# A change at the start of a hybrid attention block: which load comes second, and when the first weight piece is split

## The chip, the cores and the metric

The kernel runs on one core of one Trainium2 chip. A core has five engines with an instruction stream each: TensorE (PE, matrix products; its weight loads are shown apart as PEld), VectorE (DVE), ScalarE (ACT), GpSimd (POOL) and SyncE (SP, which here only issues DMAs). They wait for each other by semaphores. The metric is the device time of one launch in microseconds (us), lower is better.

## The reference

One layer of an encoder trunk on 256 tokens of width 2048, in float32. What matters here is its beginning: the norm of the input and one large projection.

```python
u = _rms_norm(x, norm_mix_pre[l])
mix = hybrid_mixer(u, w_in[l], ...)        # begins with proj = u @ w_in
x = x + _rms_norm(mix, norm_mix_post[l])
hdn = jnp.square(jax.nn.relu(_rms_norm(x, norm_mlp_pre[l]) @ w_mlp_up[l]))
x = x + _rms_norm(hdn @ w_mlp_down[l], norm_mlp_post[l])
```

## The kernel before, in words

A float32 product is made of three faster ones. Each operand is split into a high part (a copy rounded to the type `fp32r`, made by ScalarE) and a low part (the operand minus its high part, made by VectorE); the products high x high, high x low and low x high are added up in PSUM. For x one tile `pk` of 128 x 512 holds both parts of 128 rows of x side by side (256 tokens each), so that one matmul of 512 columns against a weight's high part `whi` makes two of the products, and one of 256 columns against its low part `wlo` makes the third.

The weights come as a stream `wst` of pieces of 128 x 1024 numbers (512 KB). The part of the program that the change touches is the first projection, of three groups of 128 output columns (`qb[0]` to `qb[2]`). Each group needs two pieces: pieces 0, 2 and 4 hold the weights for the first 1024 rows of x, pieces 1, 3 and 5 those for the rest. x comes transposed as `xt`, 16 slices `k` of 128 rows x 256 tokens, into the tile `X0`.

- Loads. `loadx(a, b)` loads slices a to b-1 of x; `load(n, q)` loads half q (512 columns, 256 KB) of piece n. SyncE's queue takes them in the order of the code, except for `loadx(0, 2)` and `loadx(2, 4)`, which ScalarE issues. SyncE waits before an issue when the semaphore that it would use belongs to a load that has not landed.
- Splits. `xsplit(k)` makes the high part (ScalarE, L242) and the low part (VectorE, L243) of slice k. The two parts of x carry the norm's gain, and the norm's factor comes later. `wpart(n, q)` does it for half q of piece n (L331, L332).
- Products. `prods(n, ks, low)` issues the matmuls of piece n for the slices `ks`: those with `whi` (L340) or those with `wlo` (L338). TensorE's order is the order of the code, since it stands under a manual schedule.
- The first loop runs over q = 0, 1, each with four slices of x and half a piece of each of the three groups. In the loop the order is: two x splits, the split of piece 0, its products with those two slices, two more x splits, their products, then pieces 2 and 4.
- Ahead of it, TensorE makes seven products of a tile of zeros, `zt`, into a PSUM bank that nobody reads (L281). Each is two matmul instructions in the trace, and 14 stand there.

All later matmuls, some 8,300 of them, follow in an order fixed by the code and by a small planner. The buffers of `whi` and `wlo` turn in threes, so the first split of piece 1 (L331, L332) writes the buffers of piece 0, and waits for TensorE's last product with them.

Of the kernel before, what the change touches and what calls it, by code (L numbers as in the profile page):

```python
# [10 lines left out]
F32 = mybir.dt.float32  # L11
F32R = mybir.dt.float32r
AF = mybir.ActivationFunctionType
ALU = mybir.AluOpType
# [3 lines left out]
T = 256  # L18
# [32 lines left out]
def hybrid_block(ctx, tc, xt, x, gains, params, consts, lora, gup, wst, out):  # L51
    nc = tc.nc
    V, A, G, PE = nc.vector, nc.scalar, nc.gpsimd, nc.tensor
# [11 lines left out]
    def nm(s):  # L65
        uid[0] += 1
        return f"{s}_{uid[0]}"

    def gps():
        return pg.tile([128, 512], F32, tag="gps", name=nm("gps"), bufs=4)  # L70

    def mps():
        return pm.tile([128, 512], F32, tag="mps", name=nm("mps"), bufs=4)

    def pk():
        return pkpool.tile([128, 512], F32R, tag="pk", name=nm("pk"), bufs=24)
# [14 lines left out]
    def P(name, i=0, r=slice(0, 128)):  # L91
        return par[r, PC[name] + i:PC[name] + i + 1]
# [143 lines left out]
    def split(src, dst, scale=None):  # L236

        if scale is None:
            A.activation(dst[:, 0:T], src, AF.Copy)
            V.tensor_tensor(dst[:, T:], src, dst[:, 0:T].bitcast(F32), ALU.subtract)  # L240
        else:
            A.activation(dst[:, 0:T], src, AF.Copy, scale=scale)  # L242
            V.scalar_tensor_tensor(dst[:, T:], src, scale, dst[:, 0:T].bitcast(F32), ALU.mult, ALU.subtract)  # L243

    def rsqrt(y, m, t):

# [19 lines left out]
    X0 = rp.tile([128, KT, T], F32, tag="SC", name="x0", bufs=1)  # L266

    def loadx(a, b, queue=nc.sync):
        return queue.dma_start(out=X0[:, a:b, :], in_=xt[:, a:b, :])

    nc.sync.dma_start(out=par, in_=params)
    for a in (0, 2):
        first_x = loadx(a, a + 2, nc.scalar)
    with tc.issue_after(first_x.ins):
        warm = A.activation(dum, dum, AF.Tanh)
    A6 = rp.tile([128, 6, T], F32, tag="b6", name="a6", bufs=1)
    zt = rp.tile([128, T], F32, tag="tha", name="zt", bufs=1)
    V.memset(zt, 0.0)
    idle = mps()
    for i in range(7):  # L280
        PE.matmul(idle[:, 0:T], zt[:, 0:128], zt, start=True, stop=True)  # L281
    raws = {}

    def load(n, q=None):

        if n not in raws:
            raws[n] = (rp.tile([128, HALF], F32, tag="m", name=nm("raw"), bufs=4) if n % 2 else
                       wpool.tile([128, HALF], F32, tag="raw", name=nm("raw"), bufs=3))
        cs = slice(0, HALF) if q is None else slice(512 * q, 512 * q + 512)
        nc.sync.dma_start(out=raws[n][:, cs], in_=wst[n][:, cs])  # L290

    for n in (0, 2, 4):
        load(n, 0)
    loadx(4, 8)
    for n in (0, 2, 4):
# [20 lines left out]

    def xsplit(k):
        u = pk()
        split(X0[:, k, :], u, P("g1", k))
        upk.append(u)  # L320

    qb = [gps() for _ in range(3)]
    w = {}

    def wpart(n, q):
        if n not in w:
            w[n] = (wpool.tile([128, HALF], F32R, tag="whi", name=nm("whi"), bufs=3),
                    wpool.tile([128, HALF], F32R, tag="wlo", name=nm("wlo"), bufs=3))
        hi, lo = w[n]
        cs = slice(512 * q, 512 * q + 512)  # L330
        A.activation(hi[:, cs], raws[n][:, cs], AF.Copy)  # L331
        V.tensor_tensor(lo[:, cs], raws[n][:, cs], hi[:, cs].bitcast(F32), ALU.subtract)  # L332

    def prods(n, ks, low):
        for k in ks:
            i = k % 8
            if low:
                PE.matmul(qb[n // 2][:, 0:T], w[n][1][:, i * 128:i * 128 + 128], upk[k][:, 0:T], start=False, stop=k == 15)  # L338
            else:
                PE.matmul(qb[n // 2], w[n][0][:, i * 128:i * 128 + 128], upk[k], start=k == 0, stop=False)  # L340

    for q in range(2):
        ks = range(4 * q, 4 * q + 4)
        for k in ks[0:2]:
            xsplit(k)
        wpart(0, q)
        prods(0, ks[0:2], False)
        for k in ks[2:4]:
            xsplit(k)
        prods(0, ks[2:4], False)  # L350
        wpart(2, q)
        prods(2, ks, False)
        prods(0, ks, True)
        wpart(4, q)
        prods(4, ks, False)
        prods(2, ks, True)
        prods(4, ks, True)
    for k in range(8, 12):
        xsplit(k)
# [66 lines left out]
    def sb_mix():  # L426
# [66 lines left out]
        for h in range(4):  # L493
            ps = mps()
            PE.matmul(ps[:, 0:256], v[0][:, h * 128:h * 128 + 128], t[:, h, 0:256], start=True, stop=False)
            PE.matmul(ps[:, 128:256], v[1][:, h * 128:h * 128 + 128], t[:, h, 256:384], start=False, stop=True)
            y = pk()
            split(ps[:, 0:256], y)
            out.append(y)
            if h % 2:  # L500
                yield 2.5
        done["ya"] = out

    def fox_mix():
# [72 lines left out]
        for h in range(4):  # L577
            ps = mps()
            PE.matmul(ps[:, 0:256], v[0][:, h * 128:h * 128 + 128], pT[:, h, 0:256], start=True, stop=False)
            PE.matmul(ps[:, 128:256], v[1][:, h * 128:h * 128 + 128], pT[:, h, 256:384], start=False, stop=True)  # L580
            y = pk()
            split(ps[:, 0:256], y)
            out.append(y)
            if h % 2:
                yield 2.5
# [453 lines left out]
    c0 = g0 + 80  # L1039
# [216 lines left out]
    for k2 in range(0, KT, 2):  # L1256
        turned(k2, 1)
        src = [trs[k2 // 2][:, i * T:i * T + T] for i in range(2)]
# [342 lines left out]
    for g in range(4):  # L1601
# [8 lines left out]
        for tt, ps in enumerate(tok(hp, 3 if g == 3 else 1)):  # L1610
# [25 lines left out]
            with tc.issue_after(added.ins):  # L1636
                for c in (1024, 1536):
                    cs = slice(c, c + 512)
# [131 lines left out]
```

## Time and profile before

| what | us |
|---|---|
| median of 3 runs | 1495.75 |
| the runs | 1493.69, 1497.37, 1495.75 |
| profiled execution, first to last instruction (the span) | 1493.8 |
| TensorE busy in it | 1480.8 |

The page gives no time of the profiled execution beside its span; the span lies 1.95 us below the median of the runs and next to the lowest of them. Busy times are sums over the instructions of an engine; a matmul's row shows its latency, and matmuls overlap, so that the distance between starts is the better measure of what one costs. All the work that the change touches lies in the first 20 us.

### The profile page before, as it was taken

The page shows a single profiled execution, that of the slowest core. Times are in us where ns is not written, and L with a number is a line of the kernel's source. Part 1 is how long each engine was busy: PE and PEld are TensorE (multiplying, and loading weights), DVE is VectorE, ACT ScalarE, POOL GpSimd, SP SyncE. Part 2 cuts the span into 40 slices and gives each one's busy share as a digit, 9 for nine tenths or more (in the row PEclk, how much of TensorE's full clock was granted, in tenths as well). Part 3 has the DMA queues.
Part 4 walks back from the last instruction along what each step waited for, and adds up shares of the span by engine and source line. Part 5 has one row for each costly group of instructions (what it writes and reads, how often), then busy time and mean ns, then how long its engine had stood idle before and what let it go on. Part 6 is the DMA issues. An engine that isn't in the chain of part 4 may idle for free.

```text
span 1493.8 us, 22852 instructions
## 1 busy us (share of the span) xinstructions
PE 1480.8 (99%) x8427; PEld 1250.7 (84%) x8427; DVE 1213.1 (81%) x1688; ACT 933.9 (63%) x1396; POOL 91.3 (6%) x160
## 2 busy tenths in 40 slices
PE   9999999999999999999999999999999999999997
PEld 8888888888778888788888888888888888888885
DVE  7666677999679798567547788999899999999996
ACT  7465666664576554474444777776766776777663
POOL 0021000100001100000000000000000000000000
PEclk9999999999999999999999999999999999999999
DMA  7545455545544545445755868888888788889874
GB/s 282 188 148 191 163 170 180 172 162 198 171 153 161 184 169 209 144 151 194 269 196 204 275 213 249 255 257 259 242 232 264 238 262 248 260 248 283 259 250 151
DMA packets 107759, 317.70 MB, mean 213 GB/s; under 512 B 10752, under 2 KB 14976, under 8 KB 107392
## 3 DMA queue, kind: packets, MB, share of 16 engines
q1 hardware_dynamic: 94688, 284.39, 54.9%
q0 software_dynamic: 8064, 29.36, 10.5%
q10 hardware_dynamic: 4896, 2.49, 0.6%
q8 instruction: 66, 1.08, 0.3%
q14 instruction: 45, 0.37, 0.1%
HBM read 282.65 MB, written 4.19 MB: 192 GB/s over the span
## 4 chain that ended last, share of the span: by engine, by line
PE 96%; DVE 1%; ACT 1%; issue 1%; POOL 0%; POOLq 0%; DVEq 0%; ACTq 0%
PE gps L220 28%; PE gps L174 23%; PE gps L178 13%; PE gps L204 7%; PE mps L1478 3%; PE mps L1479 3%; PE mps L1480 3%; PE gps L1480 3%; PE gps L1478 2%; PE gps L1479 2%; PE gps L182 2%; PE gps L340 1%; PE mps L791 1%; PE mps L281 0%; PE gps L1237 0%
## 5 line engine op out<-in xcount | busy, mean ns | idle before, releaser
L159 DVE TENSOR_TENSOR wlo<-raw,whi 128x1024 fp32r<-128x1024 f32 x497 | 602.7, 1220 | 157.2 <-ACT whi L158 140.7
L158 ACT ACTIVATE whi<-raw 128x1024 fp32r<-128x1024 f32 x497 | 522.0, 1056 | 249.7 <-PE gps L220 101.1
L174 PE MATMUL gps<-pk,whi 128*128 128x512 f32 x1336 | 336.5, 391 | 0.4 <-ACT whi L158 0.4
L174 PEld LDWEIGHTS gps<-pk,whi 128*128 128x128 f32 x1336 | 247.3, 188 | 48.8 <-ACT whi L158 0.6
L220 PE MATMUL gps<-whi,pk 128*128 128x512 f32 x1136 | 286.0, 391 | 0.0
L220 PEld LDWEIGHTS gps<-whi,pk 128*128 128x128 f32 x1136 | 211.5, 188 | 44.0
L178 PEld LDWEIGHTS gps<-pk,wlo 128*128 128x128 f32 x1424 | 194.1, 190 | 14.1 <-DVE wlo L159 0.3
L178 PE MATMUL gps<-pk,wlo 128*128 128x256 f32 x1424 | 199.3, 282 | 0.0
L220 PE MATMUL gps<-wlo,pk 128*128 128x512 f32 x568 | 155.3, 392 | 0.0
L220 PEld LDWEIGHTS gps<-wlo,pk 128*128 128x128 f32 x568 | 105.7, 188 | 21.9
L1341 DVE TENSOR_TENSOR sp<-raw,sp 128x1024 fp32r<-128x1024 f32 x67 | 81.7, 1220 | 6.7 <-ACT sp L1340 6.5
L1340 ACT ACTIVATE sp<-raw 128x1024 fp32r<-128x1024 f32 x67 | 70.6, 1054 | 19.6 <-DMA raw<-in_wst_dram 6.3
L1369 ACT ACTIVATE sp<-gps 128x512 f32<-128x512 f32 x52 | 31.1, 598 | 72.1 <-PE gps L182 72.1
L204 PE MATMUL gps<-whi,pk 128*128 128x512 f32 x256 | 68.9, 390 | 0.0
L1478 PE MATMUL mps<-whi,fm 128*128 128x512 f32 x168 | 66.1, 394 | 0.0
L1479 PE MATMUL mps<-whi,fm 128*128 128x512 f32 x168 | 65.8, 392 | 0.0
L1480 PE MATMUL mps<-wlo,fm 128*128 128x512 f32 x168 | 65.5, 390 | 0.0
L1440 POOL DMA_DIRECT2D raw<-raw x40 | 34.9, 873 | 431.1 <-DVE raw L1437 111.7
L204 PEld LDWEIGHTS gps<-whi,pk 128*128 128x128 f32 x256 | 47.8, 188 | 9.9
L1480 PE MATMUL gps<-wlo,fm 128*128 128x512 f32 x126 | 49.4, 392 | 0.5 <-DVE wlo L159 0.4
L1478 PE MATMUL gps<-whi,fm 128*128 128x512 f32 x126 | 49.2, 391 | 0.0
L1437 DVE TENSOR_TENSOR raw<-raw,raw 128x1024 f32<-128x1024 f32 x40 | 48.8, 1220 | 0.4
(393 smaller groups left out, 2009.1 us busy)
## 6 DMA issues: line engine op xcount, KB each, us to landing
raw<-in_wst_dram SPq DMA_DIRECT2D x499, 512.0 KB, 4.4
raw<-raw POOLq DMA_DIRECT2D x40, 512.0 KB, 7.6
sp<-in_wst_dram SPq DMA_DIRECT2D x16, 512.0 KB, 5.4
raw<-sp POOLq DMA_DIRECT2D x8, 512.0 KB, 6.9
sp<-raw POOLq DMA_DIRECT2D x8, 512.0 KB, 7.0
x<-in_x_dram SPq DMA_DIRECT2D x8, 256.0 KB, 5.5
xs<-x SPq DMA_DIRECT2D x2, 1024.0 KB, 4.9
x<-xs SPq DMA_DIRECT2D x4, 512.0 KB, 6.2
```

Source lines behind the costliest of these rows:

```text
L158: A.activation(hi, raw, AF.Copy)
L159: V.tensor_tensor(lo, raw, hi.bitcast(F32), ALU.subtract)
L174: PE.matmul(ps, hi[:, i * 128:i * 128 + 128], pks[i], start=first and i == 0, stop=False)
L178: PE.matmul(ps[:, 0:T], lo[:, i * 128:i * 128 + 128], pks[i][:, 0:T], start=False, stop=False)
L204: PE.matmul(ps[tt], pks[k][:, c:c + 128], w[:, (k - k0) * 512:(k - k0) * 512 + 512], start=k == 0 and part == 0 and w is hl[0], stop=w is ...
L220: PE.matmul(ps[tt], pks[k][:, c:c + 128], w[:, (k - k0) * 512:(k - k0) * 512 + 512], start=k == 0 and part == 0 and w is hl[0], stop=False)
L1340: A.activation(hi, raw, AF.Copy)
L1341: V.tensor_tensor(lo, raw, hi.bitcast(F32), ALU.subtract)
L1437: V.tensor_tensor(x, x, z, ALU.add)
L1478: PE.matmul(Q[f], p, w, start=d == 0 and i == 0, stop=False)
L1479: PE.matmul(Q[f], pl, w, start=False, stop=False)
L1480: PE.matmul(Q[f], p, wl, start=False, stop=d == nd - 1 and i == 1)
```

## The change

Four edits. The load of slices 2 and 3 of x (`loadx(2, 4)`) moves from ScalarE's queue into SyncE's, behind the first half of piece 0. The high part of that half is made in two instructions of 256 columns instead of one of 512. Its low part is made after the low parts of slices 2 and 3 instead of before them (`tc.issue_after` sets that order). And four products of zeros stand where seven stood.

```diff
     nc.sync.dma_start(out=par, in_=params)
-    for a in (0, 2):
-        first_x = loadx(a, a + 2, nc.scalar)
+    first_x = loadx(0, 2, nc.scalar)
...
-    for i in range(7):
+    for i in range(4):
         PE.matmul(idle[:, 0:T], zt[:, 0:128], zt, start=True, stop=True)
...
-    for n in (0, 2, 4):
+    load(0, 0)
+    loadx(2, 4)
+    for n in (2, 4):
         load(n, 0)
     loadx(4, 8)
...
-    def wpart(n, q):
+    def whigh(n, c0, c1):
         if n not in w:
             w[n] = (wpool.tile([128, HALF], F32R, tag="whi", name=nm("whi"), bufs=3),
                     wpool.tile([128, HALF], F32R, tag="wlo", name=nm("wlo"), bufs=3))
+        A.activation(w[n][0][:, c0:c1], raws[n][:, c0:c1], AF.Copy)
+
+    def wlow(n, c0, c1):
         hi, lo = w[n]
-        cs = slice(512 * q, 512 * q + 512)
-        A.activation(hi[:, cs], raws[n][:, cs], AF.Copy)
-        V.tensor_tensor(lo[:, cs], raws[n][:, cs], hi[:, cs].bitcast(F32), ALU.subtract)
+        V.tensor_tensor(lo[:, c0:c1], raws[n][:, c0:c1], hi[:, c0:c1].bitcast(F32), ALU.subtract)
+
+    def wpart(n, q):
+        whigh(n, 512 * q, 512 * q + 512)
+        wlow(n, 512 * q, 512 * q + 512)
...
-        wpart(0, q)
-        prods(0, ks[0:2], False)
+        if q:
+            wpart(0, q)
+            prods(0, ks[0:2], False)
+        else:
+            for i in range(2):
+                whigh(0, 256 * i, 256 * i + 256)
+            prods(0, ks[0:2], False)
         for k in ks[2:4]:
-            xsplit(k)
+            lows = xsplit(k)
         prods(0, ks[2:4], False)
+        if q == 0:
+            with tc.issue_after(lows.ins):
+                wlow(0, 0, 512)
         wpart(2, q)
```

On SyncE, the first loads of the program before the change (`raw` are the weight pieces 0, 2 and 4, 512 columns of each; `x` of 128x1024 is slices 4 to 7):

```order
L271 DMA par<-in_params_dram 128x116
L290 DMA raw_101<-in_wst_dram 128x512
L290 DMA raw_103<-in_wst_dram 128x512
L290 DMA raw_105<-in_wst_dram 128x512
L269 DMA x_85<-in_xt_dram 128x1024
```

The same place now, where `x` of 128x512 is slices 2 and 3:

```order
L271 DMA par<-in_params_dram 128x116
L289 DMA raw_97<-in_wst_dram 128x512
L269 DMA x_85<-in_xt_dram 128x512
L289 DMA raw_100<-in_wst_dram 128x512
L289 DMA raw_102<-in_wst_dram 128x512
L269 DMA x_85<-in_xt_dram 128x1024
```

Slices 2 and 3 stand behind piece 0 and ahead of pieces 2 and 4; what follows keeps its order.

On VectorE, the low parts of x (`pk`) and of the weights (`wlo`) before, from slice 0 to piece 4:

```order
L243 SCALAR_TENSOR_TENSOR pk_132<-x_85,par,pk_132 128x256
L243 SCALAR_TENSOR_TENSOR pk_135<-x_85,par,pk_135 128x256
L332 TENSOR_TENSOR wlo_139<-raw_101,whi_138 128x512
L243 SCALAR_TENSOR_TENSOR pk_144<-x_85,par,pk_144 128x256
L243 SCALAR_TENSOR_TENSOR pk_147<-x_85,par,pk_147 128x256
L332 TENSOR_TENSOR wlo_153<-raw_103,whi_152 128x512
L332 TENSOR_TENSOR wlo_165<-raw_105,whi_164 128x512
```

And now:

```order
L243 SCALAR_TENSOR_TENSOR pk_129<-x_85,par,pk_129 128x256
L243 SCALAR_TENSOR_TENSOR pk_132<-x_85,par,pk_132 128x256
L243 SCALAR_TENSOR_TENSOR pk_141<-x_85,par,pk_141 128x256
L243 SCALAR_TENSOR_TENSOR pk_144<-x_85,par,pk_144 128x256
L335 TENSOR_TENSOR wlo_136<-raw_97,whi_135 128x512
L335 TENSOR_TENSOR wlo_151<-raw_100,whi_150 128x512
L335 TENSOR_TENSOR wlo_163<-raw_102,whi_162 128x512
```

The low part of piece 0 has moved behind those of slices 2 and 3; the same seven instructions stand there. On ScalarE one instruction of 512 columns has become two of 256 in the same place, ahead of slice 2. TensorE's products stand in the order in which they stood, behind four products of zeros instead of seven, and from there to the end every engine's order is as before.

## Rows read from the trace of the kernel before

**Rows 1.** The page: busy time of each engine, share of the span, instructions.

```profile
PE 1480.8 (99%) x8427; PEld 1250.7 (84%) x8427; DVE 1213.1 (81%) x1688; ACT 933.9 (63%) x1396; POOL 91.3 (6%) x160
```

**Rows 2.** The chain that ended last, first 20 us: start, length, what.

```profile
1.18 6.33 PE mps L281 x14
...
7.98 1.84 PE gps L340 x6
...
16.36 1.84 PE gps L340 x8
```

**Rows 3.** Timeline of TensorE's matmuls: start, length, engine, line, operation, operands, count.

```profile
1.77 1.49 PE L281 MATMUL mps<-zt 128*128 128x256 f32 x3
...
6.46 1.04 PE L281 MATMUL mps<-zt 128*128 128x256 f32 x2
...
13.84 0.64 PE L338 MATMUL gps<-pk,wlo 128*128 128x256 f32 x4
...
16.19 2.00 PE L340 MATMUL gps<-pk,whi 128*128 128x512 f32 x8
```

**Rows 4.** Timeline of TensorE's weight loads, with the idle time ahead of them.

```profile
7.98 0.19 PEld L340 LDWEIGHTS gps<-pk,whi 128*128 128x128 f32 x1 [0.44 <-DVE pk L243]
8.37 1.01 PEld L340 LDWEIGHTS gps<-pk,whi 128*128 128x128 f32 x5 [0.21 <-DVE pk L243]
```

**Rows 5.** Timeline of ScalarE, from its first issues to slice 4 of x.

```profile
0.73 0.90 ACTq L269 DMA_DIRECT2D x<-in_xt_dram  x2
...
3.65 0.91 ACT L242 ACTIVATE pk<-x,par 128x256 fp32r<-128x256 f32 x2 [0.49 <-DMA x<-in_xt_dram]
6.17 0.63 ACT L331 ACTIVATE whi<-raw 128x512 fp32r<-128x512 f32 x1 [1.61 <-DMA raw<-in_wst_dram]
...
8.73 0.91 ACT L242 ACTIVATE pk<-x,par 128x256 fp32r<-128x256 f32 x2
```

**Rows 6.** Timeline of VectorE, from slice 0 of x to slice 15.

```profile
4.19 0.89 DVE L243 SCALAR_TENSOR_TENSOR pk<-x,par,pk 128x256 fp32r<-128x256 f32 x2 [0.51 <-ACT pk L242]
6.84 0.69 DVE L332 TENSOR_TENSOR wlo<-raw,whi 128x512 fp32r<-128x512 f32 x1 [1.76 <-ACT whi L331]
7.45 0.88 DVE L243 SCALAR_TENSOR_TENSOR pk<-x,par,pk 128x256 fp32r<-128x256 f32 x2
...
12.83 1.68 DVE L243 SCALAR_TENSOR_TENSOR pk<-x,par,pk 128x256 fp32r<-128x256 f32 x4
...
15.79 1.67 DVE L243 SCALAR_TENSOR_TENSOR pk<-x,par,pk 128x256 fp32r<-128x256 f32 x4
```

**Rows 7.** DMA issues, one issue each in four narrow windows: count, size, us to landing.

```profile
x<-in_xt_dram ACTq DMA_DIRECT2D x1, 256.0 KB, 2.9
...
raw<-in_wst_dram SPq DMA_DIRECT2D x1, 256.0 KB, 5.0
...
x<-in_xt_dram ACTq DMA_DIRECT2D x1, 256.0 KB, 5.2
...
x<-in_xt_dram SPq DMA_DIRECT2D x1, 512.0 KB, 6.1
```

**Rows 8.** Timeline of SyncE's issues (each `x3` has three, 0.46 apart).

```profile
1.18 1.37 SPq L290 DMA_DIRECT2D raw<-in_wst_dram  x3
2.59 0.43 SPq L269 DMA_DIRECT2D x<-in_xt_dram  x1
```

**Rows 9.** Narrow timelines of TensorE: the product of slice 2, and two weight loads.

```profile
7.98 0.50 PE L340 MATMUL gps<-pk,whi 128*128 128x512 f32 x1
...
17.35 0.41 PEld L340 LDWEIGHTS gps<-pk,whi 128*128 128x128 f32 x2
```

**Rows 10.** VectorE's wait ahead of line 332 between 13 and 15 us: ns min/median/max, start.

```profile
L332 DVEq EVENT_SEMAPHORE  x1: 859/859/859, 13.7 to 13.7; - x1
```

**Rows 11.** Table of stretches: length, busy us of the engines, PEclk, DMA share, GB/s.

```profile
1.18:7.51 6.33, 6.33 (x15) 5.01 (x16) 1.99 (x7) 3.73 (x8) 1.53 (x6) 1.00 0.89 293
...
8.38:19.00 10.62, 10.62 (x63) 9.36 (x63) 10.55 (x22) 9.88 (x22) 0.00 (x0) 1.00 1.03 421
```

More of the change, by code (lines that the diff above doesn't have):

```diff
@@ L242, in split @@
             A.activation(dst[:, 0:T], src, AF.Copy, scale=scale)
-            V.scalar_tensor_tensor(dst[:, T:], src, scale, dst[:, 0:T].bitcast(F32), ALU.mult, ALU.subtract)
+            return V.scalar_tensor_tensor(dst[:, T:], src, scale, dst[:, 0:T].bitcast(F32), ALU.mult, ALU.subtract)
     def rsqrt(y, m, t):
@@ L318, in xsplit @@
         u = pk()
-        split(X0[:, k, :], u, P("g1", k))
+        done_low = split(X0[:, k, :], u, P("g1", k))
         upk.append(u)
+        return done_low
     qb = [gps() for _ in range(3)]
     w = {}
-    def wpart(n, q):
+    def whigh(n, c0, c1):
         if n not in w:
```

## The prediction

> **What bounds the kernel now.** First the page: TensorE is busy for 1480.8 us of a span of 1493.8 [rows 1]. Only its first microseconds and the writing of the output stand outside. Then the chain of waits over the first 20 us: it runs through TensorE alone, from the zero products at 1.18 (6.33 us) to the third real product at 7.98 and on, without leaving the engine [rows 2]. Whoever wants to move the end by work at the start must move TensorE's own queue.
>
> So I read how TensorE stands to those who feed it. Its weight loads wait twice, 0.44 us ahead of slice 2's product and 0.21 ahead of slice 3's, both for the low part of x [rows 4]. Behind 8.38 it is busy for all of the stretch to 19.00 [rows 11], and for 99% of the span [rows 1]. A shift at 8.37 therefore reaches the end, unless somebody who feeds TensorE can't follow.
>
> Two such feeders are near. ScalarE starts slice 4 at 8.73 [rows 5], which is when its load lands: issue at 2.59 plus 6.1 [rows 7, 8]. Behind that, the DMA engines are full (share 1.03, 421 GB/s [rows 11]). VectorE is busy for 10.55 us of the 10.62 from 8.38 to 19.00 [rows 11]: a second queue as tight as TensorE's.
>
> **The change, part by part.**
>
> *The load order.* Piece 0's first half lands at 1.18 + 5.0 = 6.2, and ScalarE waits 1.61 us for it [rows 5, 7, 8]. Slices 2 and 3, 256 KB too, ran beside it from ScalarE's queue, issued at about 1.2 and landed after 5.2, at 6.4 [rows 5, 7]. Now piece 0 has only slices 0 and 1 and the small parameters beside it. What lands when it goes alone no row shows. Bounds: 6.2 (nothing gained), and 4.5, which is slices 0 and 1's landing (0.73 + 2.9 = 3.6 [rows 5, 7]) plus 256 KB at the stretch's 293 GB/s, 0.9 us [rows 11]. I take 5.2, in the middle. Slices 2 and 3 have the same bytes ahead as before; I take 6.3, bounds 5.9 and 6.5.
>
> *The high part in halves.* No ACTIVATE of 128x256 without a scale is in these rows; two with one take 0.91 for a pair, 512 columns 0.63 [rows 5]. So the pair costs 0.6 to 0.9, up to 0.3 more. It begins at 5.2, and ScalarE is idle until 6.3; cost 0. If piece 0 came at 6.2 after all, these 0.3 would delay slice 2.
>
> *The low part later.* This is where the gain is. Slice 3's low part now ends at 7.45 + 0.88 = 8.33, since VectorE makes piece 0's low part first, from 6.84 [rows 6]. Afterwards slice 2's low part begins 0.54 after its high part (4.19 against 3.65 [rows 5, 6]): 6.3 + 0.02 + 0.54 = 6.86, and the pair ends 0.88 later at 7.74. That is 0.59 earlier, and slice 3's product is released at 7.79 instead of 8.37: 0.58 gained for TensorE. The low part moved behind them starts at about 7.65 and ends at 8.35; its product comes after six hi products, two microseconds behind slice 3's release, so the new wait on it costs 0.
>
> *What is late next.* VectorE's queue has the same work in it and starts at 6.86 instead of 6.84, so what it makes from slice 4 on comes no earlier. The tightest meeting is slice 15: its low part ends at 15.79 + 1.67 = 17.46 [rows 6]; TensorE begins its weight load at 17.57 (17.35 + 0.41 less 0.19, the length of one [rows 4, 9]) and ends the product at 16.19 + 2.00 = 18.19 [rows 3]. A product released late ends 0.50 after its load starts [rows 9]; with 0.05 from VectorE's end to the load (8.33 becomes 8.37 [rows 4, 6]) slice 15's could end at 18.01. TensorE can come forward by 0.18 before VectorE holds it. One thing loosens this: at 13.67 VectorE began a wait of 0.86, until 14.53 [rows 10], for TensorE's last product with piece 0's low part, which ends at 13.84 + 0.64 = 14.48 [rows 3]. With an earlier TensorE it runs on from slice 11's end, at 12.83 + 1.68 = 14.51 less the 0.08 by which its instructions overlap (7.45 begins ahead of 6.84 + 0.69), and wins 0.10 [rows 6]. Together 0.28 of the 0.58 survive. With TensorE at full rate the gain is 0.28 us, bounds 0 and 0.58.
>
> *Four zero products for seven, and the clock.* Zero matmuls start 0.426 apart ((6.46 - 1.77) / 11 steps [rows 3]). Each zero product is plain float32 and stands as two matmuls in the trace. Real products of 512 columns come every 0.230 later on (1.84 / 8), and the six from 7.98 at 0.31 with the wait for slice 3 among them [rows 2]. [...]
>
> Before, TensorE was busy without a break for 6.33 us until it was at the upper level [rows 2]. Now eight zero matmuls end at about 1.77 + 6 x 0.426 + 0.6 = 4.9 (0.6 for the last one: 1.04 less 0.43 [rows 3]). Then it idles until 5.6 (piece 0 at 5.2, plus 0.4 for half a high part), makes two products, and idles again from about 6.5 to 7.4, when slice 2 is ready. When the level rises after that, no row shows. Bounds: 7.4 (no loss), and 7.4 + 6.3 = 13.7, as late after this restart as it was after the first start. In between I take 10.5, since the work before 7.4 may count in part: 3.1 us low, 3.1 x 0.46 = 1.43 lost, against 0.58 of earlier start, makes 0.85 us later than before; the break-even is a rise at 7.4 + 0.58 / 0.46 = 8.7. VectorE is then no limit any more, for TensorE arrives after it.
>
> [...]
>
> **The sum.** The profiled execution's span would go from 1493.8 to 1494.65. It lies 1.95 below the median of the runs, which spread over 3.7 us by themselves, so I lay the difference on the median: 1495.75 + 0.85 = 1496.6. For this kernel 0.3%, 4.5 us, is about what a measurement tells from no change, so I expect none to be measured.
>
> **The rivals.**
> - *The clock is up in time* (the shorter run of zeros does, or the pauses don't matter). Then the early release counts: 1495.75 - 0.28 = 1495.5. For it: the pauses are below one microsecond each. Against: 6.33 us of work stood ahead of the rise before.
> - *The DMA stream comes forward.* 293 GB/s in the first stretch against 421 later [rows 11], while two queues were served. If one queue brings the later rate from 3.6 on, 256 KB pieces land 0.3 sooner each; up to 0.6 by slice 4, and ScalarE and VectorE follow: 0.28 + 0.6, some 1494.9. Against: the first microseconds may be slow for reasons of their own.
> - *Piece 0 lands no earlier than 6.2.* ScalarE makes its halves until 7.0, slice 2 starts there, and slice 3 is released at about 8.3: 1495.7 if the clock is up; the gap behind the zeros is then 1.7 us and a late rise likelier.
> [...]
>
> **How the numbers follow.** Late rise 0.48; clock in time 0.32; DMA stream forward 0.09; piece 0 no earlier 0.08; measurably slower 0.03. The range: the late rise alone spans 1495.5 to 1498.1 (13.7: 6.3 x 0.46 - 0.58 = 2.3); the rivals reach down to 1494.9, and a median of runs that spread over 3.7 moves by over a microsecond on both sides: 1493.6 to 1498.8. Faster by over 0.3%: 0.02, from the spread alone, since no mechanism of mine reaches 4.5; slower 0.04, the last rival and the spread; within 0.3%: 0.94.
>
> **What would show it.** Right: ScalarE's first weight split before 5.6; slice 3's low part ending near 7.7; product spacing of 0.43 behind 7.4, and a place where it falls to 0.23; slice 15's product ending later than 18.19. If that spacing is 0.23 at once, the clock step is wrong, and slice 15's end should be near 17.9, held by VectorE. If piece 0 lands at 6.2, the load step is wrong. A difference of more than 3 us would come from somewhere that I have not seen, since behind 20 us no order changes.

## The result, and the profile after

| kernel | median of its runs, us | lowest and highest | runs |
|---|---|---|---|
| before | 1494.67 | 1493.35, 1497.37 | 20 |
| after | 1497.28 | 1495.47, 1499.91 | 20 |

The ratio is 1.0017, with a 95% interval of 1.0011 to 1.0023. The changed kernel is 2.6 us slower, which is less than 0.3%. The interval leaves out 1, so twenty runs of each do tell the two apart, where the prediction expected that no difference would be measured. The time is inside the predicted range and 0.7 above the predicted time; measured against the median of 20 runs of before, where the prediction had put +0.85, the difference is three times as large. That the time itself came so near is partly luck: the prediction added its +0.85 to the median of three runs, 1495.75, which was 1.1 above that of twenty. The profiled execution of after has a span of 1497.6 and took 1499.46 itself, one of the longest of the 20.

The page's first row, which answers to [rows 1], shows the same TensorE time with six matmuls fewer (the three zero products that are gone):

```profile
PE 1481.1 (99%) x8421; PEld 1251.2 (84%) x8421; DVE 1215.6 (81%) x1688; ACT 935.2 (62%) x1397; POOL 91.1 (6%) x160
```

So nothing on this row tells where the time went. The timeline of TensorE's matmuls in the first 20 us does (start, length, engine, line, operation, operands, count, idle time ahead and what ended it); it answers to [rows 3]:

```profile
1.18 3.78 PE L280 MATMUL mps<-zt 128*128 128x256 f32 x8 [1.18 <-DVE zt L277]
5.32 1.22 PE L347 MATMUL gps<-pk,whi 128*128 128x512 f32 x2 [0.36 <-ACT whi L331]
7.99 2.93 PE L347 MATMUL gps<-pk,whi 128*128 128x512 f32 x6 [1.46 <-DVE pk L243]
10.72 1.06 PE L345 MATMUL gps<-pk,wlo 128*128 128x256 f32 x4
...
14.32 2.00 PE L347 MATMUL gps<-pk,whi 128*128 128x512 f32 x8
...
18.51 2.00 PE L347 MATMUL gps<-pk,whi 128*128 128x512 f32 x8
```

TensorE pauses for 0.36 and 1.46 us. The six products from slice 2 on then take 2.93 us for what took 1.84 with a wait among it [rows 2]; four products with the low part take 1.06 instead of 0.64 [rows 3]. From 14.32 on the lengths are those of before: eight products in 2.00. The products of slices 12 to 15 start at 18.51 instead of 16.19 [rows 3], 2.32 later.

How much slower the stretch is, two rows of the table of stretches show, of nearly equal length, with TensorE busy throughout and full DMA engines in both (columns: length, busy us and instructions of PE, PEld, DVE, ACT, POOL; PEclk, DMA share, GB/s):

```profile
8.00:13.30 5.30, 5.30 (x15) 4.32 (x16) 5.09 (x11) 4.68 (x10) 0.00 (x0) 1.00 1.03 411
13.30:18.50 5.20, 5.20 (x33) 4.69 (x32) 3.82 (x10) 4.42 (x11) 0.00 (x0) 1.00 1.03 420
```

Fifteen matmuls in the first, 33 in the second, and a granted clock of 1.00 in both. The list of the granted clock that the trace holds, from which the table takes this column, explains the 1.00: its first entry, of 1.00, begins at 13.45 us here (in before at 7.36), and the table counts the time ahead of the first entry as 1.00. So the trace does record the rise, and it stands where the spacing changes: products of 512 columns start every 0.43 us from 8.59 to 13.28 (the lower level) and every 0.23 us from 14.32 on (the upper).

The chain of the first 20 us answers to [rows 2]. It no longer stays in TensorE: it goes through the load of slices 2 and 3 and their split.

```profile
1.64 5.25 DMA x<-in_xt_dram
...
6.91 0.52 ACT pk L242
...
7.45 0.50 DVE pk L243
...
7.99 2.93 PE gps L347 x6
```

The feeders: ScalarE, which answers to [rows 5], then VectorE, which answers to [rows 6] (timelines).

```profile
4.87 0.71 ACT L331 ACTIVATE whi<-raw 128x256 fp32r<-128x256 f32 x2
6.91 0.91 ACT L242 ACTIVATE pk<-x,par 128x256 fp32r<-128x256 f32 x2 [1.34 <-DMA x<-in_xt_dram]
...
9.78 0.91 ACT L242 ACTIVATE pk<-x,par 128x256 fp32r<-128x256 f32 x2 [0.61 <-DMA x<-in_xt_dram]
```

```profile
7.45 0.88 DVE L243 SCALAR_TENSOR_TENSOR pk<-x,par,pk 128x256 fp32r<-128x256 f32 x2 [1.98 <-ACT pk L242]
8.25 1.89 DVE L335 TENSOR_TENSOR wlo<-raw,whi 128x512 fp32r<-128x512 f32 x3
```

Piece 0's halves are made 1.3 us sooner than its high part was. The low parts of slices 2 and 3 begin at 7.45, exactly where they began before, although piece 0's low part has left its place ahead of them: their load came at 6.89, and [rows 5] have it by 6.7. Slice 4 starts 1.05 later than at 8.73 [rows 5]. SyncE's issues, which answer to [rows 8], have part of the reason:

```profile
1.17 0.42 SPq L289 DMA_DIRECT2D raw<-in_wst_dram  x1
1.64 0.42 SPq L269 DMA_DIRECT2D x<-in_xt_dram  x1
2.11 0.91 SPq L289 DMA_DIRECT2D raw<-in_wst_dram  x2
3.06 0.84 SPq L269 DMA_DIRECT2D x<-in_xt_dram  x1
```

The load of slices 4 to 7 is issued at 3.06 instead of 2.59 [rows 8], since one more issue stands ahead of it.

In this execution the end lies 3.8 us behind that of before (spans 1497.6 and 1493.8), and 2.32 of it are there at 20 us. The chain shows the same 2.32 at 98.58, the first product behind a stall far from the change (rows of before, and of after):

```profile
98.58 1.88 PE gps L174 x7
```

```profile
100.90 1.89 PE gps L174 x7
```

Part of the remaining 1.5 shows in the page's row on the products of line 174, for which TensorE sat idle 1.3 us in all, while in a second profile of the same kernel (run e9, below) it was 0.4 (columns: count, busy us and mean ns, idle before and its releaser). The row of after, and that of its repetition:

```profile
L174 PE MATMUL gps<-pk,whi 128*128 128x512 f32 x1336 | 336.6, 392 | 1.3 <-DVE junk L1500 1.0
```

```profile
L174 PE MATMUL gps<-pk,whi 128*128 128x512 f32 x1336 | 336.5, 392 | 0.4 <-ACT whi L158 0.4
```

So that wait comes and goes between executions of one kernel. It is not the only one. Product by product, TensorE in after is 2.3 us behind before up to 680 us, 2.6 at 1197 and 3.8 from 1393 on; in the thirteen profiles of changed kernels this lag moves by between -1.8 and +1.2 us from 1197 to 1396, by stalls that are there in one execution and not in another, in e4 for instance, which has the loads of before:

```profile
1333.74 0.50 PE L1494 MATMUL gps<-wlo,fm 128*128 128x512 f32 x1 [1.10 <-DVE wlo L159]
```

The end of a single profile therefore says little about the first 20 us; the place at 98.58 says more. As to line 174's wait, in the profiles of the runs below it stands in three more with the new load order (e1, e5, e12), and in none of the four kernels with the old one; ten against four are too few to say that the load order brings it.

### The profile page after: what moved, and what is told of

It is laid out like the page before. It is cut to its first block, busy times and chain, and to the rows that moved or that the text cites. A ratio compares the mean times of both kernels' runs of the same rounds, so it can differ in the third digit from the quotient of the medians.

```text
span 1497.6 us, 22840 instructions
## 1 busy us (share of the span) xinstructions
PE 1481.1 (99%) x8421; PEld 1251.2 (84%) x8421; DVE 1215.6 (81%) x1688; ACT 935.2 (62%) x1397; POOL 91.1 (6%) x160
## 3 DMA queue, kind: packets, MB, share of 16 engines
q0 software_dynamic: 8064, 29.36, 10.5%
## 4 chain that ended last, share of the span: by engine, by line
PE 91%; issue 3%; DMA 2%; DVE 2%; ACT 1%; POOL 1%; POOLq 0%; DVEq 0%; SPq 0%; ACTq 0%
PE gps L220 28%; PE gps L174 21%; PE gps L178 12%; PE gps L204 7%; PE mps L1493 3%; PE mps L1494 3%; PE mps L1495 3%; PE gps L1495 2%; PE gps L1493 2%; PE gps L1494 2%; PE gps L182 1%; DMA raw<-raw 1%; DVE wlo L159 1%; PE gps L347 1%; PE mps L806 1%
## 5 line engine op out<-in xcount | busy, mean ns | idle before, releaser
L174 PE MATMUL gps<-pk,whi 128*128 128x512 f32 x1336 | 336.6, 392 | 1.3 <-DVE junk L1500 1.0
L174 PEld LDWEIGHTS gps<-pk,whi 128*128 128x128 f32 x1336 | 247.3, 188 | 49.9 <-ACT pk L1394 1.4
```

The lines of the kernel that those rows point to most:

```text
L174: PE.matmul(ps, hi[:, i * 128:i * 128 + 128], pks[i], start=first and i == 0, stop=False)
```

## The experiments

The theory, an estimate of the author's (the clock theory of the expectations): TensorE reaches slice 2 at the lower level because a shorter run of zero products and two pauses put the rise off, and the lost time is kept to the end. The rivals: the new load order delays the feeders (the load theory); the splits in new places cost; the loss arises further back. Each run's profile is one execution, its median eleven or twelve (after's twenty). The column "rise" is where the first entry of the granted clock begins in the profiled execution (before: 7.36). The last column is by how much the chain's `L174 x7` starts later than at 98.58 in the one profiled execution. Each is compared with runs of before on the same chip; the ratio is not exactly the quotient of the medians.

| run | zero products | median, us | minus before's, us | ratio, 95% interval | rise, us | at 98.58, us |
|---|---|---|---|---|---|---|
| after | 4 | 1497.28 | +2.61 | 1.0017 [1.0011, 1.0023] | 13.45 | +2.32 |
| e9, after again | 4 | 1496.67 | +1.23 | 1.0008 [0.9999, 1.0017] | 10.58 | +0.66 |
| e10 | 0 | 1497.10 | +1.66 | 1.0013 [1.0004, 1.0021] | 9.77 | +0.48 |
| e7 | 5 | 1496.27 | +1.09 | 1.0005 [0.9996, 1.0014] | 6.16 | +0.33 |
| e12 | 6 | 1496.00 | +0.56 | 1.0008 [0.9999, 1.0016] | 4.64 | +0.30 |
| e1 | 7 | 1495.23 | +0.27 | 1.0003 [0.9994, 1.0012] | 5.18 | +0.22 |
| e5 | 4, 2 in the pause | 1496.46 | +1.28 | 1.0007 [0.9999, 1.0016] | 5.28 | +0.02 |
| e6 | 5, 2 in the pause | 1494.92 | -0.26 | 1.0001 [0.9992, 1.0010] | 5.08 | +0.22 |
| e11 | as e6, more moved | 1495.51 | +0.07 | 1.0002 [0.9993, 1.0010] | 5.04 | -0.03 |
| e2, before with | 4 | 1496.25 | +1.29 | 1.0008 [0.9999, 1.0017] | 5.33, fall at 8.75 | +1.38 |
| e3, loads alone | 7 | 1495.65 | +0.69 | 1.0004 [0.9996, 1.0013] | 4.91 | +0.30 |
| e4, splits alone | 7 | 1495.34 | +0.38 | 1.0000 [0.9991, 1.0009] | 5.01 | +0.11 |
| e8, as e4, more moved | 7 | 1494.90 | -0.28 | 1.0002 [0.9993, 1.0011] | 6.20 | +0.02 |

**e1: the change with seven zero products.**

```diff
-    for i in range(4):
+    for i in range(7):
         PE.matmul(idle[:, 0:T], zt[:, 0:128], zt, start=True, stop=True)
```

> The changed kernel with seven zero products instead of four, all else as changed. [...] Load theory (the DMA stream that runs 1 us late from slice 4 on is what costs): the time stays at +2.5. [...]

The loss is nearly gone: +0.27. TensorE's matmuls, and the waits of its weight loads (timelines):

```profile
1.18 5.25 PE L280 MATMUL mps<-zt 128*128 128x256 f32 x14 [1.18 <-DVE zt L277]
...
7.84 1.83 PE L347 MATMUL gps<-pk,whi 128*128 128x512 f32 x6 [0.95 <-DVE pk L243]
...
16.05 2.35 PE L347 MATMUL gps<-pk,whi 128*128 128x512 f32 x8
```

```profile
8.24 1.00 PEld L347 LDWEIGHTS gps<-pk,whi 128*128 128x128 f32 x5 [0.21 <-DVE pk L243]
17.11 0.19 PEld L347 LDWEIGHTS gps<-pk,whi 128*128 128x128 f32 x1 [0.17 <-DVE pk L243]
17.51 0.19 PEld L347 LDWEIGHTS gps<-pk,whi 128*128 128x128 f32 x1 [0.21 <-DVE pk L243]
17.90 0.19 PEld L347 LDWEIGHTS gps<-pk,whi 128*128 128x128 f32 x1 [0.21 <-DVE pk L243]
```

The six products take 1.83, the upper level, though a pause of 0.95 stood ahead of them. Slice 3 is released 0.13 sooner than at 8.37 [rows 4], and by slices 13 to 15 TensorE waits for VectorE three times: the group ends at 18.40, behind the 18.19 of before [rows 3]. That is the hold of the prediction's rival with the clock up in time, and it takes more than was gained. As far as these medians go, the loss hangs on the three zero products; the other three edits together give nothing back.

**e2: the kernel before with four zero products.**

```diff
-    for i in range(7):
+    for i in range(4):
         PE.matmul(idle[:, 0:T], zt[:, 0:128], zt, start=True, stop=True)
```

> The kernel before with four zero products instead of seven and nothing else. Clock theory: zeros end at 4.9, first product at 6.9, then products 0.43 apart until some point between 9 and 14; +1.0 to +3.0 us. Load theory: the loads are as before, so 0.0 within 0.5.

With this one edit, old loads and old splits, the median is 1.29 above before's (the interval just takes in 1), and the profile has +1.38 at 98.58. Here the clock did something else than in after. TensorE's matmuls, then three stretches:

```profile
6.71 0.73 PE L340 MATMUL gps<-pk,whi 128*128 128x512 f32 x2 [1.74 <-ACT whi L331]
7.83 2.48 PE L340 MATMUL gps<-pk,whi 128*128 128x512 f32 x6 [0.39 <-DVE pk L243]
10.10 1.06 PE L338 MATMUL gps<-pk,wlo 128*128 128x256 f32 x4
...
13.38 2.00 PE L340 MATMUL gps<-pk,whi 128*128 128x512 f32 x8
```

```profile
6.71:8.70 1.99, 1.60 (x5) 0.91 (x6) 1.99 (x5) 1.79 (x4) 0.00 (x0) 1.00 0.99 355
8.70:12.10 3.40, 3.40 (x12) 2.85 (x11) 3.36 (x8) 3.28 (x8) 0.00 (x0) 0.51 1.05 417
12.10:16.00 3.90, 3.90 (x24) 3.42 (x24) 2.50 (x7) 3.11 (x8) 0.00 (x0) 0.99 1.03 420
```

The first two products take 0.73 (1.22 in after), so the upper level was reached; the rise is on record at 5.33, in the pause between 4.96 and 6.71, right behind the zeros. Then, 0.9 us into work that had resumed at 7.83, the granted clock falls to 0.51 for 3.4 us. What it did before the fall: a pause of 1.74, two products, a pause of 0.39. The low-part products of that stretch take 1.06, as in after's, where the table says 1.00: it is the same level. The trace has an entry for this fall (8.75 to 12.16) but none for a start at the lower level.

**e3 and e4: the load order alone, and the two split edits alone,** each with seven zero products. e3 against before:

```diff
-    for a in (0, 2):
-        first_x = loadx(a, a + 2, nc.scalar)
+    first_x = loadx(0, 2, nc.scalar)
...
-    for n in (0, 2, 4):
+    load(0, 0)
+    loadx(2, 4)
+    for n in (2, 4):
         load(n, 0)
```

e4 is the rest: `whigh` and `wlow`, the halves of piece 0 and `tc.issue_after`, word for word as in the change.

> The kernel before with the load of slices 2 and 3 moved into SyncE's queue behind piece 0, seven zeros, splits as before. Load theory: slice 4 lands at 9.7 instead of 8.7 and everything of ScalarE and VectorE comes 1 us later; if that alone is the cost, +2.5, and by slice 15's meeting with TensorE +0.8. [...]

> The kernel before with the high part in halves and piece 0's low part behind slices 2 and 3, loads and seven zeros as before. My sum: slice 3's low part ends at about 8.2 instead of 8.33, since the halves delay slice 2's high part by 0.1 to 0.3; -0.1 us, between -0.3 and +0.1, which is below what can be measured. If these edits carried the loss, +2.5.

Neither can be told from before. In e3's profile slices 4 to 7 come at 9.41, about as late as in e1 (9.32); in e4's, with the loads of before, at 9.22. In both slice 3 is released earlier than at 8.37 (8.20 and 8.14, weight loads), and in both VectorE holds slices 13 to 15, in e3 at 17.20, 17.60 and 17.99, in e4 so (waits of its weight loads):

```profile
17.01 0.19 PEld L346 LDWEIGHTS gps<-pk,whi 128*128 128x128 f32 x1 [0.18 <-DVE pk L243]
17.40 0.19 PEld L346 LDWEIGHTS gps<-pk,whi 128*128 128x128 f32 x1 [0.21 <-DVE pk L243]
17.80 0.19 PEld L346 LDWEIGHTS gps<-pk,whi 128*128 128x128 f32 x1 [0.21 <-DVE pk L243]
```

So the loads and the splits each release slice 3 sooner in these executions, and neither gets the gain past slice 15.

**e5 and e6: zero products in the pause.** e5 puts two of them between the products of slice 1 and slice 2 of the changed kernel; e6 does the same and has five in front.

```diff
             prods(0, ks[0:2], False)
+            for i in range(2):
+                PE.matmul(idle[:, 0:T], zt[:, 0:128], zt, start=True, stop=True)
```

> The changed kernel with two more zero products between the products of slice 1 and slice 2 (four in front, two there). They fill the wait of 1.5 us from 6.5 to 8.0; the pause of 0.36 ahead of the first product stays. [...]

> As the run with the bridge, with five zero products in front instead of four, so that TensorE has no pause from 1.2 to slice 2's product. [...]

e6 brings the loss back to nothing (-0.26) with the changed loads and splits. e6's matmuls:

```profile
1.18 4.33 PE L280 MATMUL mps<-zt 128*128 128x256 f32 x10 [1.18 <-DVE zt L277]
5.88 0.74 PE L347 MATMUL gps<-pk,whi 128*128 128x512 f32 x2 [0.36 <-ACT whi L331]
6.45 1.03 PE L361 MATMUL mps<-zt 128*128 128x256 f32 x4
7.37 1.83 PE L347 MATMUL gps<-pk,whi 128*128 128x512 f32 x6
```

Slice 2 begins 0.6 earlier than in before, its product has no pause ahead of it (the 0.36 ahead of the first product is still there), and it runs at the upper level. The rise stands at 5.08 here and at 5.28 in e5, ahead of the two products in the pause (6.45 and 6.15): in these two profiles the filled pause can have kept the level, but did not raise it. None of it is left at the end: VectorE holds TensorE at slices 13 to 15 again, and the group ends at 15.94 + 2.46 = 18.40. e5 doesn't fit as well: in its one profile the upper level is there with the first product (0.72 for the pair) and `L174 x7` starts 0.02 late, yet this execution took 1496.92 and the median is +1.28. It has the idle 1.4 us ahead of line 174's products that after has. So its loss, in this execution at least, was not the clock's. Of the others only the mean granted clock is on record, to three places: 7 of the 11 timed runs stand at 0.997, against 8 of the 33 of before beside them. A fall like e2's takes 0.0011 off this mean (an estimate: 3.4 us at 0.50, of 1494). The last microseconds of an execution, which the list has at 0.50 too (5.1 us in before, 6.2 in after), move the third place as well, so this is a hint at such falls, not a measurement.

**e7, e12 and e10: five, six and no zero products** in the changed kernel. The edit of e7 and e12 is that of e1 with 5 and 6; e10 drops the loop and its bank.

```diff
-    idle = mps()
-    for i in range(4):
-        PE.matmul(idle[:, 0:T], zt[:, 0:128], zt, start=True, stop=True)
```

> The changed kernel with five zero products instead of four, without a bridge: no pause ahead of the first product, only the one ahead of slice 2 (6.7 to 7.9, about 1.2 us). Theory that the length of the first run decides: 5.5 us of it lift the clock ahead of slice 2 and the time is +0.1 to +0.5. Theory that the pause decides: products stay 0.43 apart behind it for some microseconds, +0.8 to +2.5.

> The changed kernel with six zero products instead of four. Dose: with 4 zeros +2.5 us, with 5 +1.1, with 7 +0.3 were measured. [...] If the pause ahead of slice 2 did harm by itself, they would give as much as 5, +1.1.

> The changed kernel with no zero products. TensorE's first work is the product of slice 0 at 5.3, and it pauses again until slice 2 at 8.0. If the four zeros do nothing for the clock, the time is that of the change, +2.0 to +3.0 us. If they lift it in a part of the executions, it is +2.5 to +4, above the change, with every timed run late.

The cost falls from five over six to seven products, +1.09, +0.56, +0.27, each step smaller than the intervals. With none it is +1.66, between the two measurements of four: in the medians, four zero products are worth nothing that shows as starters of the clock, though in e2 and e5 the rise came right behind them. The profiles of e7 and e10 are the second fastest of their kernels' executions (1494.67 and 1495.15), so their place at 98.58 may not be a typical one. Two rows, of e12 and of e10:

```profile
7.96 1.80 PE L347 MATMUL gps<-pk,whi 128*128 128x512 f32 x6 [1.76 <-DVE pk L243]
```

```profile
7.67 2.62 PE L344 MATMUL gps<-pk,whi 128*128 128x512 f32 x6 [0.30 <-DVE pk L243]
```

e12's products are at the upper level behind a pause of 1.76; e10's six begin at the lower one and change over while they run, near 9.7, the first product having begun at 6.15. A pause alone doesn't decide, then. With five to seven zeros in front the rise came by 7.4 in all nine profiles, before among them, and none fell again in the first 20 us; with four it came at 5.3, 5.3, 10.6 and 13.5, and one of the early ones fell.

**e9: the changed kernel again,** without an edit.

> The changed kernel once more, for a second execution's clock. If the rise at 13.3 us is what its four zeros and two pauses always lead to, the profile shows spacing 0.43 from 8 to 11 or later again, and the median stays +2.0 to +3.0 us. If where the clock rises moves from execution to execution, this profile may show it earlier, and the timed runs spread over 3 us or more with the median still +1.5 to +3.

+1.23 instead of +2.61; the intervals of the ratios overlap. TensorE's matmuls, and its weight loads from slice 2 on:

```profile
6.15 4.16 PE L347 MATMUL gps<-pk,whi 128*128 128x512 f32 x8 [1.18 <-ACT whi L331]
10.10 0.85 PE L345 MATMUL gps<-pk,wlo 128*128 128x256 f32 x4
10.80 1.08 PE L347 MATMUL gps<-pk,whi 128*128 128x512 f32 x4
```

```profile
7.37 2.21 PEld L347 LDWEIGHTS gps<-pk,whi 128*128 128x128 f32 x6 [0.72 <-DVE pk L243]
```

Here slices 0 to 3 all run at the lower level (4.16 us for eight products), and the four from 10.80 at the upper. The rise came at 10.58, and at 13.45 in after's first profile. The same program pays 0.66 or 2.32 in two executions; besides the rise, slice 2's start moved too (7.37 and 7.99).

**e8 and e11: the hold of VectorE.** e8 is e4 with the second low part of piece 1 made behind the low parts of slices 12 to 15; e11 is e6 with the same.

```diff
-    for q in range(2):
-        wpart(1, q)
+    wpart(1, 0)
+    whigh(1, 512, 1024)
...
-        xsplit(k)
+        lows = xsplit(k)
+    with tc.issue_after(lows.ins):
+        wlow(1, 512, 1024)
```

> The kernel before with loads and seven zeros as before, the split edits of the change, and besides the low part of piece 1's second half moved behind the low parts of slices 12 to 15. My theory that VectorE's queue holds TensorE at slices 13 to 15: those weight loads no longer wait, slice 15's product ends near 17.9 instead of 18.2 to 18.4, and all that follows comes 0.1 to 0.4 us earlier than before; in the time -0.3, not to be told from 0. If another feeder takes over at once, 0.

> The changed kernel with five zeros in front, two between slices 1 and 2, and the low part of piece 1's second half behind slices 12 to 15: both pauses filled and VectorE's hold at slice 15 taken away. Clock theory with VectorE's queue as next limit: slice 15's product ends at 17.6 to 18.1, time -0.4 to +0.1 us against before. If the loads, which in this order ran some 0.6 us later from slice 4 on, hold slices 4 to 7 instead, 0.0 to +0.3.

In e8 the three waits are gone, but piece 0 came at 6.3 in its profiled execution, slice 3 was released at 8.40, and nothing was there to keep. In e11 slice 3 is released at 8.09, and one wait is left by slices 12 to 15, whose products are these:

```profile
16.01 2.14 PE L347 MATMUL gps<-pk,whi 128*128 128x512 f32 x8
```

It ends at 18.15 (before 18.19 [rows 3]) and `L174 x7` starts at 98.55, 0.03 ahead. Neither median can be told from before's. No version here beats before by more than can be measured.

## Why the prediction came out as it did

**The forecast, later by a late clock, was right in its main step.** In both profiles of the changed kernel the rise is on record 3 to 6 us later than in before, and TensorE is late by what that costs. Restoring the zeros (e1), or five zeros in front with two more in the pause ahead of slice 2 (e6), takes the loss away with the other edits in place, and removing three zeros from before (e2) brings one in without them, though the intervals of single runs touch or overlap. Of the thirteen measurements, the seven with fewer than seven zero products that don't follow e6 (after, e9, e10, e7, e12, e5, e2) lie at +1.4 us on the mean of the table's medians, the six others (e1, e3, e4, e6, e8, e11) at +0.15. The spacing of 0.43 us at the lower level was right: 2.93 us for six products, as 5 x 0.43 plus the last one's length. No row of before gives the 0.46 of the sum, the share of its time that TensorE loses at the lower level; in after the spacings of 0.427 and 0.230 make it 1 - 0.230 / 0.427 = 0.46. The 1.00 of [rows 11] doesn't show the level at the start; the trace's list does, by where it begins (7.36 in before). That pauses put the rise off was the author's estimate, and no run shows it by itself: e12 has its rise at 4.64 and keeps the level over a pause of 1.76.

**The term that was mis-sized is the rise.** It was put at 10.5, between bounds of 7.4 and 13.7. The first profile has it at 13.45, close to the upper bound, and none of the earlier start of 0.58: from 7.99 on that is 5.46 us x 0.46 = 2.5, less the 0.2 of the stall ahead of slice 3 that no longer binds, and 2.32 was measured. The second has it at 10.58 with the earlier start as forecast (7.37): 3.21 x 0.46 = 1.48, less 0.61 and the same 0.2, makes 0.67, and 0.66 was measured, near the predicted 0.85. The sum's one gap there is that stall. So 10.5 was a fair single value, but a kernel with an uncertain rise is timed over many executions, and its medians, +2.6 and +1.2 us in two measurements, lie above what the value in the middle gives. How much of them is the rise and how much the later waits, the medians don't separate.

**A second way of losing was not in the prediction.** In e2 the rise came in time, at 5.33, and the level was lost again at 8.75. The mean granted clock of the timed runs hints that this is not rare: it is 0.997 or less in 40 of the 64 timed runs of the five measurements with four or five zeros and a pause (after, e9, e2, e5, e7), and in 35 of the 190 others that have it on record. Of the four slowest runs of after, 1499.2 to 1499.9, three have 0.998, too high for a fall like e2's; the profiled one, with its late rise, is among these three.

**The load order.** Piece 0 landed at 1.18 + 3.5 = 4.7, sooner than the 5.2 that I took (4.5 at best); 4.6 in e3, 5.5 in e9. Two things were wrong. Slices 2 and 3 were to land at 6.3 with "the same bytes ahead"; ScalarE starts them at 6.91 here, outside the bounds. Over the ten profiles with the new order it starts at 6.3 to 6.9, over the four with the old one at 6.6 to 6.9, where its own work sets some of these starts: the order makes no difference that these show, the scatter does. And for slices 4 to 7 the sum had no term at all: ScalarE begins them at 9.3 on the mean of ten profiles, at 8.9 on that of four. The issue that comes 0.47 later is of this size; that it is the cause was not tried apart.

**The DMA stream didn't come forward.** The table of stretches of after and of before (same stretches) speaks against that rival:

```profile
3.18:5.18 2.00, 1.78 (x5) 0.87 (x3) 1.02 (x5) 1.13 (x4) 0.00 (x0) 1.00 0.96 253
5.18:7.18 2.00, 1.22 (x2) 0.50 (x2) 0.30 (x1) 0.66 (x3) 0.00 (x0) 1.00 0.95 237
```

```profile
3.18:5.18 2.00, 2.00 (x6) 1.53 (x5) 1.32 (x5) 0.91 (x2) 0.00 (x0) 1.00 0.98 309
5.18:7.18 2.00, 2.00 (x7) 1.62 (x5) 0.34 (x1) 1.00 (x3) 0.00 (x0) 1.00 1.03 366
```

With one queue instead of two, 253 and 237 GB/s stand against 309 and 366. In e9 the second figure was 360, so this too belongs to the execution.

**The halves** cost 0.71 us as a pair and stand ahead of ScalarE's wait of 1.34: nothing, as forecast.

**The low part later** was to release slice 3 0.58 sooner. In after it gave 0, since its load came late; slice 3 was released 0.13 sooner in e1, 0.23 in e4 and 0.6 in e6, but also 0.17 in e3, which hasn't this edit, so the scatter of the loads is part of these gains. What the sum said of the rest held in each of these: VectorE's queue, not TensorE's, sets slice 15, and the gain ends there. It even turned over, 18.40 against a forecast of near 17.9, because VectorE itself was later with slices 4 to 7 coming later (it began slice 4 at 9.91 in e1 and at 9.44 in before, and had no break from there to slice 15). e8 and e11 loosen that hold: the three waits are gone in e8, and one is left in e11. That a gain was behind it they don't show.

**The piece-0 rival** (no earlier than 6.2) didn't occur, nor did the measurably slower case, the last rival of the chances. By the prediction's own numbers that case takes a loss of 4.5 + 0.58 = 5.1 us, 11 us at the lower level (5.1 / 0.46), and so a rise at 18.5 (7.4 + 11.1), an estimate; the latest on record is 13.45.

**Open:** why, with four zeros in front, the rise comes at 5.3 in one execution and at 10.6 or 13.5 in another, and what loses it again. e12 and e1 kept the upper level over pauses of 1.76 and 0.95, e2 lost it after pauses of 1.74 and 0.39, and only one execution of each was recorded.

## What to carry to other kernels

Work that seems idle at the start of a kernel, as products nobody reads, may bear on when TensorE's clock rises: here by 7.4 us in all nine profiles with five to seven zero products in front, at 5.3 to 13.5 in the four with four. Before any of it is cut, price the first microseconds at both spacings, here 0.43 and 0.23 us. A gain at one engine's wait reached here only as far as the next queue that was as full (in e1 slice 3 came 0.13 sooner, and the waits for VectorE at slices 13 to 15, of 0.17 to 0.21, took it back): look for such a queue in the same table of stretches before the gain is booked. And where an effect depends on when the clock rises, one profile shows a possibility, not the mean: two profiles of one kernel differed by 1.7 us at 98.58 here, and only medians of many runs ranked the versions, roughly at that.

## What the runs showed of the hardware

- In these runs the trace's list of the granted clock begins with the first rise: at 13.45 us in after, 10.58 in e9, 9.77 in e10, where the spacing of the products changes from 0.43 us to 0.23. Ahead of that entry the table of stretches shows 1.00 (8.00 to 13.30 in after), while a later fall has an entry of its own (0.51 from 8.70 to 12.10 in e2, where the products take as long as in after). The start at the lower level had to be read from the first entry or from the spacing here; in after, e9 and e10 the two agree to within 0.2 us.
- With zero products unbroken from 1.18 us on, five to seven of them, the rise came between 4.64 and 7.36 us in nine profiles; with four, at 5.28 to 13.45.
- The upper level was lost again in one profile: in e2 it fell at 8.75, 0.9 us into resumed work, behind pauses of 1.74 and 0.39. e12, with a single pause of 1.76 and no fall there, shows that the length of a pause alone doesn't tell when.
- The same loads land up to a microsecond apart in two executions of the same program: piece 0 at 4.7 and 5.5, slices 4 to 7 at 9.8 and 8.8 in after and e9.
